# Attention q and k by slices, every second modulation row on VectorE, gates and one value set as channels

## The chip, the cores and the metric

One core of a Trainium2 chip runs the whole program. The metric is device time in microseconds (us), lower is better, and it counts one execution from its start to its end. Five engines work side by side, each through its own list of instructions in a fixed order: TensorE (PE; its weight loads are PEld), VectorE (DVE), ScalarE (ACT), GpSimd (POOL) and SyncE (SP), which issues the large DMAs. An engine whose next instruction has to wait does nothing behind it either.

## The reference

One decoder layer on 256 tokens of width 2048, all in float32. `c` is the conditioning vector.

```python
mod = (silu(c) @ ada_w + ada_b)                      # 2048 x 12288
sh1, sc1, g1, sh2, sc2, g2 = split(mod, 6)
h = rmsnorm(x, norm1_g) * (1 + sc1) + sh1
proj = h @ w_in                                      # 2048 x 5392
aq, ak, av, bq, bk, bv, bz, bb, ba, cq, ck, cv = split(proj)
o_a = dilated_attention(aq, ak, av)                  # 8 heads, three patterns
o_b = gated_deltanet(bq, bk, bv, bz, bb, ba)         # 4 key heads, 8 value heads
o_c = windowed_attention(cq, ck, cv, sinks)          # 8 heads, 2 key/value heads
x = x + g1 * (concat(o_a, o_b, o_c) @ w_out)         # 2048 x 2048
h = rmsnorm(x, norm2_g) * (1 + sc2) + sh2
x = x + g2 * moe(h)                                  # 32 experts, each token uses 2
return rmsnorm(x, final_norm_g)
```

`ada_w` is 100 MB; its first two sixths (sh1, sc1) are needed before anything else, the other four (g1, sh2, sc2, g2, called rows 0 to 3 below) only from the output projection on. The experts' weights are some 400 MB and all are read.

## The kernel before

**Stages.** (1) The slices: the normed input is made and projected in six slices of its 2048 channels (`SLICES`), which need the matching columns of sh1 and sc1 only. In `first`, tiles of `ada_w` (`ada_items`) alternate with tiles of `w_in` (`win_items`, L205). This stage makes only the columns of B (the gated DeltaNet): q, k, v by `chans`, and the 16 gate columns by `gate_columns` when a slice's first tile is at hand. Each slice's part sums are added to an SBUF tile on VectorE (`evac`, L271); the first slice is copied on ScalarE. (2) The rest of `w_in`, 256 columns at a time over all 2048 channels (`win_pair`, two loads of 1 MB each): A's q, k, v (`a_cols`), C's q, k, v (`c_cols`), B's z (`z_cols`). `KINDS` says which columns come out as channels (weights stationary, 256 tokens moving: `w<-stg,hx 128x256`) and which as tokens (`w<-hx,stg`; C's values are 128 wide, so they are matmuls of 128x128). Beside them run the DeltaNet (`delta`, a long chain of small matmuls through PSUM banks of tag "d") and the attention (`attention(0)` for A, `attention(1)` for C). (3) The output projection W_out by `wout_part`, in two halves of its input channels: qs (0, 3) for A's and C's heads and then qs (1, 2) for the DeltaNet's heads. (4) The router, and the experts to the end.

**A weight** is loaded in float32 and made into a high and a low part of float32r by `split` (ScalarE casts, L289; the rest by a subtraction on VectorE or POOL, L290), and each product is three matmuls (`mm3`). In the trace one matmul of a float32 operand is two records.

**The rows.** The four rows g1, sh2, sc2, g2 are 64 tiles of 1 MB (`ada_rows(i, kt)`: row i, channel block kt of 128). `row_tile` (L421 on) does one with four matmuls of 32x512, `prow<-ring,csil`, accumulated over kt in the one bank of tag "r"; after kt = 15 VectorE adds the bank to the SBUF tile `mrow` (L433), and row 2 also makes `n2row` (L435). The loads go through an own stream `st2` with two slots, "rc0" and "rc1" of 1 MB (`side`), which the slices use first and then hand over. `rows_q` lists the tiles row after row; 24 of them are merged with the A columns, 12 with C's, 20 with z's, and the last 8 stand two by two behind the four parts of W_out's first half. `mrow` has to be whole when it is turned for the router (`a<-ident,mrow`), just ahead of W_out's second half.

**What sets the order.** The program is written as a list, and a scheduler with a timeline of its own fixes each engine's order when the kernel is built. Slots and banks are given out in program order: a tile that asks for a bank of a tag waits for the tile that had the bank before it by program order, however far that one's work is put back. `delta()` is called ahead of the merged columns and rows, so that all its "d" banks come ahead of whatever asks for "d" there. `BANKS` gives three banks to "d", three to "w", one each to "a" and "r".

Of the kernel before, what the change touches and what calls it, by code (L numbers as in the profile page):

```python
# [8 lines left out]
F32 = mybir.dt.float32  # L9
# [27 lines left out]

SLICES = [(0, 2), (256, 2), (512, 4), (1024, 4), (1536, 2), (1792, 2)]

PAIRS = [c for a, e in ((O_AQ, O_BQ), (O_CQ, N_IN), (O_BZ, O_BB)) for c in range(a, e, 256)]  # L40

EARLY = ([("ada", s, k0, nk, q) for k0, nk in SLICES for s in range(2) for q in range(nk)]
         + [("b", k0, nk, c) for k0, nk in SLICES for c in range(O_BQ, O_BZ, 2048 // nk)]
         + [("pair", c, h) for c in PAIRS for h in range(2)]
         + [("out", n, q) for n in range(4) for q in range(4)])

# [2 lines left out]
def hybrid_moe(ctx: ExitStack, tc: tile.TileContext, x, c, norm1_g, norm2_g, early, ada_w, ada_b, w_bb,  # L49
# [14 lines left out]
    def mm(o, lhsT, rhs, start=True, stop=True):  # L64
        return T.matmul(o, lhsT, rhs, start=start, stop=stop, skip_group_check=True)  # L65
# [37 lines left out]
    def bank(tag, bufs=None, name=None):  # L103
        return psum.tile([P, 512], F32, name=name or tag, tag=tag, bufs=bufs or BANKS[tag])
# [98 lines left out]

    def win_items(j):
        k0, nk = SLICES[j]  # L205
        return [(early_load("b", k0, nk, c), lambda t, a=(k0, nk, c): win_tile(*a)(t)) for c in range(O_BQ, O_BZ, 2048 // nk)]

    def on(s, items):
        return [(s, load, fn) for load, fn in items]
# [16 lines left out]
    for nk, r in ((4, 4), (2, 8)):  # L226
# [6 lines left out]
        for k0, n in SLICES:  # L233
            if n == nk:
# [8 lines left out]


    CH = [("aq0", 0, 2), ("aq1", 2, 2), ("ak0", 4, 2), ("ak1", 6, 2), ("bq", 8, 4), ("bk", 12, 4),
          ("bv0", 16, 4), ("bv1", 20, 4), ("cq0", 24, 2), ("cq1", 26, 2), ("ck", 28, 1)]
    chan = {}
    K_BZ, K_BB, K_CV = 0, 1024, 1040

    KINDS = [(O_AQ, O_AV, "chan", 0), (O_AV, O_BQ, "av", 0), (O_BQ, O_BZ, "chan", 8), (O_BZ, O_BB, "tok", K_BZ),  # L250
             (O_CQ, O_CV, "chan", 24), (O_CV, N_IN, "tok", K_CV)]

    def ep_tile(tag, n, dt=F32):
        return ep.tile([P, n, NB, P], dt, name=tag, tag=tag)
# [102 lines left out]
    def win_tile(k0, nk, c0):  # L357

        def chans(w, cc, m):

            h = hs[k0]
            p = bank("w")
            for u in range(2):
                for kt in range(nk):
                    mm3(p[:, 256 * u:256 * u + 256], [x[:, kt, cc + P * u:cc + P * (u + 1)] for x in w],
                        [x[:, kt] for x in h], kt == 0, kt == nk - 1)
            t, i = chan[m]
            evac(t[:, i:i + 2].rearrange("p m b t -> p (m b t)"), p, k0)

        def gate_columns():  # L370
            h = hs[k0]
            for b in range(NB):
                p = bank("w")
                for kt in range(nk):
                    mm3(p[:, 0:16], [x[:, kt, P * b:P * (b + 1)] for x in h], [x[:, k0 // P + kt] for x in wbb],
                        kt == 0, kt == nk - 1)
                evac(tok[:, b, K_BB:K_BB + 16], p[:, 0:16], k0)

        def f(t):
            t = t.rearrange("p (k n) -> p k n", k=nk)  # L380
            n = 1024 // nk
            for a in range(0, 2048 // nk, n):
                w = split(t[:, :, a:a + n], nk, 0)
                for z in range(0, n, 256):
                    chans(w, z, 8 + (c0 - O_BQ + a + z) // P)
            if c0 == O_BQ:
                gate_columns()
        return f
# [32 lines left out]


    rowp = {}

    def row_tile(i, kt):
        def f(t):
            if kt == 0:
                rowp[i] = bank("r", name="prow2")
            for g in range(4):
                mm(rowp[i][32 * g:32 * g + 32, :], csil[:, kt, 3 - i:35 - i], t[:, 512 * g:512 * (g + 1)],  # L430
                   start=(kt == 0), stop=(kt == 15))
            if kt == 15:
# [15 lines left out]
            mm(p, identr[q, 32 * g + i:32 * g + i + 1].to_broadcast([32, P]), h[q], start=(j == 0), stop=(j == 1))  # L448


    rows_q = [(ada_rows(i, kt), row_tile(i, kt)) for i in range(4) for kt in range(KT)]

    st2 = Stream()

# [12 lines left out]

    rows_q = on(st2, rows_q)
    a_cols, c_cols, z_cols = ([x for c0 in range(a, e, 256) for x in on(st, win_pair(c0))]
                              for a, e in ((O_AQ, O_BQ), (O_CQ, N_IN), (O_BZ, O_BB)))  # L470
    w_items = [(early_load("out", n, q), None) for qs in ((0, 3), (1, 2)) for n in range(4) for q in qs]
    for s, load, _ in a_cols + c_cols + z_cols + on(st, w_items) + rows_q:
        s.add(load)
# [101 lines left out]
    st.retire(*spare)  # L575
    for s in side:
        st.retire(s, to=st2)
    st.grow((wk, "rx"))
    use(first[-8:])


# [80 lines left out]
    def attention(grp):  # L662
        if grp:
            swap_keys()
            clo = ep_tile("av", 4, F32R)
        for j in range(2):
            ms = (2 * j, 2 * j + 1)
            sd = [attn_scores(grp, m) for m in ms]
            pair = (ep_tile(f"cq{j}", 2, F32R), clo[:, 2 * j:2 * j + 2]) if grp else \
                (ep_tile(f"aq{j}", 2, F32R), ep_tile(f"ak{j}", 2, F32R))  # L670
            for i, m in enumerate(ms):
                mix[m if grp == 0 else 12 + m] = tuple(t[:, i] for t in pair)
                attn_values(grp, m, *sd[i])


    def delta():
# [726 lines left out]
```

## Time and profile before

| | us |
|---|---|
| median of 3 runs | 1641.44 (1640.99 to 1648.26) |
| the profiled execution | 1645.27 |
| its span | 1643.4 |
| delta's last matmuls start | 442.1 |
| last z column ends, W_out starts | 532.4 |
| `mrow` gets its last row | 600.1 |
| `mrow` turned for the router | 604.0 |
| first matmul of an expert | 683.4 |

The page lists busy time by engine, then the span in 40 slices (41 us each). In PE's timeline a row is a start, a duration and a count of records of one form; since matmuls overlap, what a group costs is read from start to the next row's start.

### The profile page before, as it was taken

Reading aid. Unit: us, or ns where it says so; the run is one execution under the profiler, and the core shown is the slowest. Engines: PE = TensorE matmul, PEld = TensorE weight load, DVE = VectorE, ACT = ScalarE, POOL = GpSimd, SP = SyncE. Lnnn points to the kernel's source line nnn. Section 1 sums busy time; section 2 is a strip of 40 time slices with the busy share of each in tenths; the row PEclk is TensorE's granted clock in tenths of the full one; section 3 lists DMA queues with packets and bytes.
Section 4 is the critical chain, followed back from the end, with each engine's and each line's share of the span. In section 5 each row is a group of like instructions: output and inputs, shape, how many; then the busy total and the mean of one; then the engine's idle time right before and its main releaser. Section 6 shows DMA issues by size and latency. Waiting matters only on the chain. (4 is left out here: it accounts for less than half of the span.)

```text
span 1643.4 us, 23829 instructions
## 1 busy us (share of the span) xinstructions
PE 1545.9 (94%) x10064; PEld 945.0 (58%) x10064; DVE 672.1 (41%) x1138; ACT 398.6 (24%) x683; POOL 182.8 (11%) x104
## 2 busy tenths in 40 slices
PE   5899899999999999799999999999999999999895
PEld 3678767898877667544544545445445445445433
DVE  3534854334433544423432533344244234235324
ACT  3323563344345334210110110111011101101102
POOL 1111222352222432000000000000000000000000
PEclk8999999999999999799999999999999999999998
DMA  9986457634589894699999999999999999999995
GB/s 392 408 329 237 162 206 293 246 155 161 225 309 315 308 369 178 232 397 421 420 419 421 421 420 421 421 420 420 421 420 421 420 421 421 421 421 421 420 420 218
DMA packets 82437, 573.76 MB, mean 349 GB/s; under 512 B 9740, under 2 KB 10100, under 8 KB 13336
## 3 DMA queue, kind: packets, MB, share of 16 engines
q1 hardware_dynamic: 82080, 572.02, 86.6%
q8 instruction: 81, 1.33, 0.3%
q10 hardware_dynamic: 248, 0.19, 0.0%
q14 instruction: 28, 0.23, 0.0%
HBM read 570.07 MB, written 2.10 MB: 348 GB/s over the span
## 5 line engine op out<-in xcount | busy, mean ns | idle before, releaser
L65 PE MATMUL u<-ring,xg 128*64 128x512 f32 x2048 | 485.9, 604 | 7.8 <-DMA ring<-in_expert_gu_dram 7.8
L65 PEld LDWEIGHTS u<-ring,xg 128*64 128x64 f32 x2048 | 134.3, 137 | 236.1 <-issue 190.5
L65 PE MATMUL d<-ring,hidT 128*64 128x256 f32 x2048 | 238.1, 382 | 10.5 <-DMA ring<-in_expert_dn_dram 8.9
L65 PE MATMUL w<-hx,stg 128*128 128x256 f32 x1392 | 197.1, 293 | 9.8 <-ACT stg L289 3.1
L65 PEld LDWEIGHTS w<-hx,stg 128*128 128x128 f32 x1392 | 176.6, 194 | 41.8 <-issue 24.3
L65 PEld LDWEIGHTS d<-ring,hidT 128*64 128x64 f32 x2048 | 144.0, 137 | 90.9 <-issue 10.3
L290 POOL TENSOR_TENSOR stg<-ring,stg 128x1024 fp32r<-128x1024 f32 x53 | 128.3, 2421 | 410.5 <-ACT stg L289 367.3
L289 ACT CAST stg<-ring 128x1024 fp32r<-128x1024 f32 x116 | 121.2, 1047 | 187.7 <-PE w L65 152.4
L1190 DVE TENSOR_TENSOR xt<-xt,s 128x512 f32<-128x512 f32 x120 | 82.6, 688 | 165.2 <-PE s L65 164.4
L290 DVE TENSOR_TENSOR stg<-ring,stg 128x1024 fp32r<-128x1024 f32 x63 | 82.2, 1306 | 104.5 <-ACT stg L289 103.7
L1174 DVE SCALAR_TENSOR_TENSOR z<-d,gs,g2b 64x512 f32<-64x512 f32 x120 | 90.0, 750 | 76.1 <-PE d L65 74.2
L65 PE MATMUL prow<-ring,csil 128*32 128x512 f32 (+1 forms) x896 | 113.3, 566 | 0.3 <-DVE csil L180 0.3
L1272 POOL TENSOR_TENSOR xf<-xt,fgb 128x1024 f32<-128x1024 f32 x1 | 2.4, 2377 | 954.9 <-SPq L1289 954.9
L1107 DVE TENSOR_TENSOR xg<-g,sh2c 128x512 f32<-128x512 f32 x64 | 43.6, 691 | 136.8 <-PE u L65 75.7
L65 PEld LDWEIGHTS w<-stg,hx 128*128 128x128 f32 x672 | 83.6, 189 | 22.3 <-issue 18.0
L65 PE MATMUL w<-stg,hx 128*128 128x256 f32 (+1 forms) x672 | 96.1, 288 | 0.0
L1146 ACT ACTIVATE hid<-u 64x512 f32<-64x512 f32 x32 | 18.9, 590 | 286.7 <-PE u L65 276.5
L65 PEld LDWEIGHTS s<-yah,wt 128*128 128x128 f32 x120 | 22.6, 188 | 97.6 <-issue 58.8
L1177 ACT CAST yah<-z 64x512 fp32r<-64x512 f32 x60 | 37.0, 617 | 166.8 <-DVE z L1174 166.8
L1147 DVE TENSOR_TENSOR hid<-hid,u 64x512 f32<-64x512 f32 x32 | 22.1, 690 | 134.0 <-ACT hid L1146 133.8
L65 PE MATMUL g<-oh,h2hi 128*128 128x256 f32 x256 | 70.2, 307 | 5.5 <-DVE xg L1107 4.8
L1121 ACT CAST wt<-t 128x512 fp32r<-128x512 f32 x16 | 9.4, 587 | 233.7 <-PE s L65 222.6
(387 smaller groups left out, 1704.6 us busy)
## 6 DMA issues: line engine op xcount, KB each, us to landing
ring<-in_expert_gu_dram SPq DMA_DIRECT2D x256, 1024.0 KB, 19.8
ring<-in_expert_dn_dram SPq DMA_DIRECT2D x128, 1024.0 KB, 19.8
ring<-in_early_dram SPq DMA_DIRECT2D x90, 1024.0 KB, 8.2
ring<-in_ada_w_dram SPq DMA_DIRECT2D x64, 1024.0 KB, 5.7
xt<-in_x_dram SPq DMA_DIRECT2D x8, 512.0 KB, 6.3
out_dram<-xt SPq DMA_DIRECT2D x8, 256.0 KB, 4.4
fgb<-in_final_norm_g_dram SPq DMA_DIRECT2D x1, 1024.0 KB, 19.8
rw<-in_router_w_dram SPq DMA_DIRECT2D x1, 320.0 KB, 5.2
```

The lines of the kernel that those rows point to most:

```text
L65: return T.matmul(o, lhsT, rhs, start=start, stop=stop, skip_group_check=True)
L289: S.copy(hi, src)
L290: (G if nsplit[0] % GS[part] == GS[part] - 1 else V).tensor_tensor(lo, src, hi, op=ALU.subtract)
L1107: V.tensor_tensor(self.xg[:, 2 * q:2 * q + 2, 0:w], p[:, 0:2 * w].rearrange("p (k s) -> p k s", k=2), sh2c.rearrange("p n k -> p (n k)")[: ...
L1121: S.copy(self.wt.rearrange("p h b t -> p (h b t)"), p)
L1146: S.activation(hid[64:128], p[0:64], AF.Silu)
L1147: V.tensor_tensor(hid[0:64], hid[64:128], p[64:128], op=ALU.mult)
L1174: V.scalar_tensor_tensor(o.rearrange("p (n j) -> p n j", n=m), pd[q, 0:256 * m].rearrange("p (n j) -> p n j", n=m), gs[q, h, u:u + 1], g2h ...
L1177: S.copy(ys[h][q, c], o)
L1190: V.tensor_tensor(x1[n][:, b], x1[n][:, b], p, op=ALU.add)
L1272: G.tensor_tensor(xf, x1[0], fgb[:, None, 0:512].to_broadcast([P, NB, 512]), op=ALU.mult)
```

## The change

- `SLICED`: A's q and k (1024 columns) move from the column stage into the slices: 8 of 1 MB more among the 16 tiles of `w_in` there. They are summed slice by slice through `evac` like B's.
- `gate_columns` makes the gates as channels: 48 matmuls of 16x256 in place of 96 of 128x16, and two transposes in `delta`, which now ask for a "d" bank.
- C's values are channels too (`KINDS`): 48 matmuls of 128x256 in place of 96 of 128x128, and two transposes and a copy in `swap_keys`.
- Rows 0 and 2 are summed on VectorE (`on_dve`): each tile is two operations on 128x1024, a product with the tile's column of `csil` added to an SBUF tile `racc`, which has one buffer. After kt = 15 four matmuls with `onec` sum over the partitions into a bank of tag "d". Rows 1 and 3 stay on PE.
- `rows_q` goes by pairs: rows 0 and 1 alternate, then rows 2 and 3. Attention is a generator in pieces, and the columns, the attention's pieces and the first 56 row tiles are merged evenly. The third extra slot "rx" of the column stream is gone.

```diff
-PAIRS = [c for a, e in ((O_AQ, O_BQ), (O_CQ, N_IN), (O_BZ, O_BB)) for c in range(a, e, 256)]
+PAIRS = [c for a, e in ((O_AV, O_BQ), (O_CQ, N_IN), (O_BZ, O_BB)) for c in range(a, e, 256)]
+SLICED = [(O_BQ, O_BZ), (O_AQ, O_AV)]
...
-    KINDS = [(O_AQ, O_AV, "chan", 0), (O_AV, O_BQ, "av", 0), (O_BQ, O_BZ, "chan", 8), (O_BZ, O_BB, "tok", K_BZ),
-             (O_CQ, O_CV, "chan", 24), (O_CV, N_IN, "tok", K_CV)]
+    KINDS = [(O_AV, O_BQ, "av", 0), (O_BZ, O_BB, "tok", K_BZ), (O_CQ, N_IN, "chan", 24)]
...
         def gate_columns():
             h = hs[k0]
-            for b in range(NB):
-                p = bank("w")
-                for kt in range(nk):
-                    mm3(p[:, 0:16], [x[:, kt, P * b:P * (b + 1)] for x in h], [x[:, k0 // P + kt] for x in wbb],
-                        kt == 0, kt == nk - 1)
-                evac(tok[:, b, K_BB:K_BB + 16], p[:, 0:16], k0)
+            p = bank("w")
+            for kt in range(nk):
+                mm3(p[0:16, 0:256], [x[:, k0 // P + kt] for x in wbb], [x[:, kt] for x in h], kt == 0, kt == nk - 1)
+            evac(bbT, p[0:16, 0:256], k0)
...
+        def on_dve(t):
+            if kt == 0:
+                rowp[i] = wk.tile([P, D], F32, name="racc", tag="racc")
+            acc = rowp[i]
+            for h in range(2):
+                c = slice(1024 * h, 1024 * (h + 1))
+                if kt == 0:
+                    V.tensor_scalar(acc[:, c], t[:, c], csil[:, kt, 3:4], None, op0=ALU.mult)
+                else:
+                    V.scalar_tensor_tensor(acc[:, c], t[:, c], csil[:, kt, 3:4], acc[:, c], op0=ALU.mult, op1=ALU.add)
+            if kt == 15:
+                rowp[i] = bank("d", name="prow2")
+                for g in range(4):
+                    mm(rowp[i][32 * g:32 * g + 32, :], onec[:, 3 - i:35 - i], acc[:, 512 * g:512 * (g + 1)])
+
+        def f(t):
+            (on_pe if i % 2 else on_dve)(t)
             if kt == 15:
                 V.tensor_tensor(mrow, mrow, rowp.pop(i), op=ALU.add)
...
-    rows_q = [(ada_rows(i, kt), row_tile(i, kt)) for i in range(4) for kt in range(KT)]
+    rows_q = [(ada_rows(i, kt), row_tile(i, kt)) for i0 in (0, 2) for kt in range(KT) for i in (i0, i0 + 1)]
...
-    st.grow((wk, "rx"))
...
+        p = bank("a")
+        for b in range(NB):
+            T.transpose(p[:, P * b:P * (b + 1)], head(29)[:, b], ident)
+        S.copy(tok[:, :, K_CV:K_CV + 128], p[:, 0:256].rearrange("p (b n) -> p b n", b=NB))
...
-    use(merge(a_cols, rows_q[0:24]))
-    attention(0)
-    use(merge(c_cols, rows_q[24:36]))
-    attention(1)
-    use(merge(z_cols, rows_q[36:56]))
+    parts = [attention(grp) for grp in range(2)]
+    steps = a_cols + merge(c_cols, parts[:1] * 8) + merge(z_cols, parts[1:] * 8)
+    for step in merge(steps, rows_q[0:56]):
+        if isinstance(step, tuple):
+            use([step])
+        else:
+            next(step)
```

**PE at the end of delta.** `d<-t,qk` is delta's work; the tiles `prow` with `csil` are row tiles, a number for each row's bank (before: 4112 is row 2, 4889 row 3; after: 3279 is row 1, 4285 row 3), and `prow` with `racc` is the finish of a row that VectorE summed (4229 is row 0, 5418 row 2). Before, from delta's last values on:

```order
L65 MATMUL d<-t_2736,Um 128x128 x4
L65 MATMUL w<-stg,hx 128x128 x21
L65 MATMUL prow_4112<-ring,csil 32x512 x5
L65 MATMUL d<-t_2745,qk 128x128 x4
L65 MATMUL prow_4112<-ring,csil 32x512 x3
L65 MATMUL w<-hx,stg 128x256 x12
L65 MATMUL w<-stg,hx 128x128 x24
L65 MATMUL w<-hx,stg 128x256 x12
L65 MATMUL w<-stg,hx 128x128 x24
L65 MATMUL prow_4112<-ring,csil 32x512 x4
L65 MATMUL a<-ck,ident 64x256 x2
L65 MATMUL w<-stg,hx 128x256 x11
```

After, from delta's last values to the start of the second half of A's heads in W_out:

```order
L67 MATMUL d<-t_3195,Um 128x128 x4
L67 MATMUL w<-stg,cq_4869 128x512 x4
L67 MATMUL w<-stg,av 128x512 x2
L67 MATMUL d<-t_3204,qk 128x128 x4
L67 MATMUL prow_4229<-racc,onec 32x512 x4
L67 MATMUL prow_4285<-ring,csil 32x512 x4
L67 MATMUL w<-t_5066,identr 128x512
L67 MATMUL w<-t_5067,identr 128x512
L67 MATMUL w<-stg,aq_3697 128x512 x2
```

The finish of row 0 stands right behind delta's last matmuls, and the first tile of row 3 behind that; the last tile of row 1 stands 167 rows of this list further up. Between them there is no row tile. In the kernel before row tiles stand all along.

**PE at the end of W_out's first half.** Names with bq, bk, bv are the second half's (one of its four parts stands ahead). Before, the last two row tiles; `a<-ident,mrow` comes 12 rows of the list further on:

```order
L65 MATMUL w<-stg,bq 128x512
L65 MATMUL prow_4889<-ring,csil 32x512 x4
L65 MATMUL w<-stg,bq 128x512
L65 MATMUL w<-stg,bk 128x512
L65 MATMUL w<-stg,bq 128x512 x2
L65 MATMUL w<-stg,bk 128x512
L65 MATMUL w<-stg,bq 128x512
L65 MATMUL prow_4889<-ring,csil 32x512 x4
L65 MATMUL w<-stg,bq 128x512 x2
```

After, up to the turn of `mrow`:

```order
L67 MATMUL w<-stg,bv_5009 128x512
L67 MATMUL w<-stg,bv_5008 128x512 x2
L67 MATMUL w<-stg,bv_5009 128x512
L67 MATMUL prow_4285<-ring,csil 32x512 x28
L67 MATMUL prow_5418<-racc,onec 32x512 x4
L67 MATMUL prow_4285<-ring,csil 32x512 x8
L67 MATMUL a<-ident,mrow 128x4 x4
L67 MATMUL w<-g1hl,identr 128x512 x4
L67 MATMUL a<-rsum,ones 128x40
```

Nine tiles of row 3 (28 matmuls, then 8) and the finish of row 2 now stand in one block between the two halves. Seven tiles stand further up, the first where the piece above shows it, the six others in W_out's first half.

**SP, the queue of the loads, at the start of W_out.** `in_ada_w` are the row tiles' loads, `in_early` those of columns and W_out, `in_x` the input once more. Before:

```order
L188 DMA ring<-in_ada_w_dram 128x2048 [waits DMAHW4_49,PE_49]
L188 DMA ring<-in_ada_w_dram 128x2048 [waits DMAHW5_49,DMAHW0_49,PE_49]
L185 DMA ring<-in_early_dram 128x2048 [waits DVE_49,Pool_49]
L944 DMA xt_5118<-in_x_dram 128x2x512 [waits PE_49]
L944 DMA xt_5119<-in_x_dram 128x2x512 [waits DMAHW3_49,PE_49]
L188 DMA ring<-in_ada_w_dram 128x2048 [waits DMAHW7_49,PE_49]
L944 DMA xt_5120<-in_x_dram 128x2x512 [waits PE_49]
L188 DMA ring<-in_ada_w_dram 128x2048 [waits DMAHW6_49,DMAHW0_49,PE_49]
```

After:

```order
L980 DMA xt_5001<-in_x_dram 128x2x512 [waits PE_49]
L187 DMA ring<-in_early_dram 128x2048 [waits DMAHW4_49,DVE_49,Pool_49]
L187 DMA ring<-in_early_dram 128x2048 [waits DMAHW5_49,DVE_49,Pool_49]
L187 DMA ring<-in_early_dram 128x2048 [waits DMAHW6_49,DVE_49,Pool_49]
L190 DMA ring<-in_ada_w_dram 128x2048 [waits DVE_49]
L190 DMA ring<-in_ada_w_dram 128x2048 [waits DMAHW7_49,PE_49]
L190 DMA ring<-in_ada_w_dram 128x2048 [waits DMAHW6_49,DMAHW0_49,DVE_49]
L190 DMA ring<-in_ada_w_dram 128x2048 [waits DMAHW7_49,DMAHW1_49,PE_49]
L190 DMA ring<-in_ada_w_dram 128x2048 [waits DMAHW2_49,DMAHW0_49,DVE_49]
L187 DMA ring<-in_early_dram 128x2048 [waits DMAHW3_49,DVE_49,Pool_49]
L190 DMA ring<-in_ada_w_dram 128x2048 [waits DMAHW4_49,DMAHW1_49,PE_49]
L190 DMA ring<-in_ada_w_dram 128x2048 [waits DMAHW5_49,DMAHW2_49,DVE_49]
```

Before, each row load waits for PE alone. After, the first of the 30 last row loads stands behind the loads of x, and the loads wait for DVE and PE in turn: each of the two slots is loaded again when its own row's engine is done with it.

## Rows read from the trace of the kernel before

**Rows 1.** The page: share of the span by engine; GB/s of DMA in 40 slices.

```profile
span 1643.4 us, 23829 instructions
...
PE 1545.9 (94%) x10064; PEld 945.0 (58%) x10064; DVE 672.1 (41%) x1138; ACT 398.6 (24%) x683; POOL 182.8 (11%) x104
...
GB/s 392 408 329 237 162 206 293 246 155 161 225 309 315 308 369 178 232 397 421 420 419 421 421 420 421 421 420 420 421 420 421 420 421 421 421 421 421 420 420 218
```

**Rows 2.** Stretches of 50 us: busy us and count by engine, granted clock, DMA share.

```profile
core 0: us, PE busy (x) PEld busy (x) DVE busy (x) ACT busy (x) POOL busy (x), PEclk, DMA share, GB/s
...
200.00:250.00 50.00, 45.68 (x305) 32.67 (x306) 30.61 (x49) 30.40 (x50) 14.39 (x8) 0.97 0.61 211
...
550.00:600.00 50.00, 50.00 (x243) 30.36 (x242) 18.64 (x23) 16.40 (x18) 14.39 (x6) 1.00 0.86 315
600.00:650.00 50.00, 50.00 (x233) 37.68 (x234) 22.78 (x32) 23.82 (x35) 17.41 (x8) 1.00 0.65 252
```

**Rows 3.** PE in order of time, around delta's last matmuls: start us, us.

```profile
442.13 1.16 PE L65 MATMUL d<-t,qk 128*128 128x128 f32 x8
...
449.83 2.79 PE L65 MATMUL w<-stg,hx 128*128 128x128 f32 x24
452.55 1.07 PE L65 MATMUL prow<-ring,csil 128*32 128x512 f32 x8
453.55 0.65 PE L65 MATMUL a<-ck,ident 128*64 128x256 f32 x4
...
464.07 3.30 PE L65 MATMUL w<-stg,hx 128*128 128x256 f32 x26
467.31 0.92 PE L65 MATMUL a<-ck,cq 64*128 64x128 f32 x4
```

**Rows 4.** PE in order of time: gate columns; W_out matmuls; mrow turned.

```profile
185.50 1.40 PE L65 MATMUL w<-wbb,hx 128*128 128x16 f32 x12
187.64 7.91 PE L65 MATMUL w<-hx,stg 128*128 128x256 f32 x52 [0.73 <-DVE bk L271]
...
532.43 0.40 PE L65 MATMUL w<-stg,aq 128*128 128x512 f32 x1
...
591.08 0.40 PE L65 MATMUL w<-stg,av 128*128 128x512 f32 x1
591.32 0.40 PE L65 MATMUL w<-stg,cq 128*128 128x512 f32 x1
...
603.96 0.95 PE L65 MATMUL a<-ident,mrow 128*128 128x4 f32 x8
```

**Rows 5.** All uses of mrow, 190 to 700 us: ns min/median/max, first and last start.

```profile
L433 DVE TENSOR_TENSOR mrow<-mrow,prow x4: 675/684/689, 292.0 to 600.1; 128x512 f32<-128x512 f32 x4
```

**Rows 6.** Issues of the row loads, by window: KB, median us to landing.

```profile
ring<-in_ada_w_dram SPq DMA_DIRECT2D x1, 1024.0 KB, 4.7
...
ring<-in_ada_w_dram SPq DMA_DIRECT2D x8, 1024.0 KB, 5.0
...
ring<-in_ada_w_dram SPq DMA_DIRECT2D x16, 1024.0 KB, 5.6
...
ring<-in_ada_w_dram SPq DMA_DIRECT2D x10, 1024.0 KB, 6.5
```

**Rows 7.** Groups on VectorE, 190 to 700 us: busy us, mean ns of one.

```profile
L290 DVE TENSOR_TENSOR stg<-ring,stg 128x1024 fp32r<-128x1024 f32 x42 | 54.7, 1302 | 100.3 <-ACT stg L289 99.6 <-PE prow L65 0.6
...
L1060 DVE SCALAR_TENSOR_TENSOR h2lo<-xa,r,h2hi 128x512 fp32r<-128x512 f32 x8 | 5.7, 747 | 1.0 <-ACT h2hi L1009 1.0
```

**Rows 8.** VectorE and POOL in order of time, 194 us on.

```profile
194.58 2.29 DVE L696 SCALAR_TENSOR_TENSOR ct<-bk,cw,ct 128x255 f32<-128x255 f32 x1 [0.20 <-ACT ct L691]
...
201.06 0.47 DVE L696 SCALAR_TENSOR_TENSOR ct<-bk,cw,ct 128x254 f32<-128x254 f32 x1
...
194.22 2.38 POOL L290 TENSOR_TENSOR stg<-ring,stg 128x1024 fp32r<-128x1024 f32 x1 [5.04 <-ACT stg L289]
```

**Rows 9.** A stretch at the router's end: columns as in Rows 2.

```profile
677.00:683.00 6.00, 5.67 (x26) 5.67 (x27) 2.29 (x5) 0.59 (x1) 0.00 (x0) 0.50 0.25 107
```

More of the change, by code (lines that the diff above doesn't have):

```diff
@@ L38 @@
 SLICES = [(0, 2), (256, 2), (512, 4), (1024, 4), (1536, 2), (1792, 2)]
-PAIRS = [c for a, e in ((O_AQ, O_BQ), (O_CQ, N_IN), (O_BZ, O_BB)) for c in range(a, e, 256)]
+PAIRS = [c for a, e in ((O_AV, O_BQ), (O_CQ, N_IN), (O_BZ, O_BB)) for c in range(a, e, 256)]
+SLICED = [(O_BQ, O_BZ), (O_AQ, O_AV)]
 EARLY = ([("ada", s, k0, nk, q) for k0, nk in SLICES for s in range(2) for q in range(nk)]
-         + [("b", k0, nk, c) for k0, nk in SLICES for c in range(O_BQ, O_BZ, 2048 // nk)]
+         + [("b", k0, nk, c) for k0, nk in SLICES for a, e in SLICED for c in range(a, e, 2048 // nk)]
          + [("pair", c, h) for c in PAIRS for h in range(2)]
@@ L205, in win_items @@
         k0, nk = SLICES[j]
-        return [(early_load("b", k0, nk, c), lambda t, a=(k0, nk, c): win_tile(*a)(t)) for c in range(O_BQ, O_BZ, 2048 // nk)]
+        return [(early_load("b", k0, nk, c), lambda t, a=(k0, nk, c): win_tile(*a)(t)) for s, e in SLICED for c in range(s, e, 2048 // nk)]
     def on(s, items):
@@ L245, in hybrid_moe @@
     CH = [("aq0", 0, 2), ("aq1", 2, 2), ("ak0", 4, 2), ("ak1", 6, 2), ("bq", 8, 4), ("bk", 12, 4),
-          ("bv0", 16, 4), ("bv1", 20, 4), ("cq0", 24, 2), ("cq1", 26, 2), ("ck", 28, 1)]
+          ("bv0", 16, 4), ("bv1", 20, 4), ("cq0", 24, 2), ("cq1", 26, 2), ("ck", 28, 1), ("cv", 29, 1)]
     chan = {}
     K_BZ, K_BB, K_CV = 0, 1024, 1040
-    KINDS = [(O_AQ, O_AV, "chan", 0), (O_AV, O_BQ, "av", 0), (O_BQ, O_BZ, "chan", 8), (O_BZ, O_BB, "tok", K_BZ),
-             (O_CQ, O_CV, "chan", 24), (O_CV, N_IN, "tok", K_CV)]
+    KINDS = [(O_AV, O_BQ, "av", 0), (O_BZ, O_BB, "tok", K_BZ), (O_CQ, N_IN, "chan", 24)]
     def ep_tile(tag, n, dt=F32):
@@ L259, in hybrid_moe @@
             chan[m0 + i] = (t, i)
+    bbT = ep.tile([P, 256], F32, name="bbT")[0:16]
     av = ep.tile([P, NB, 512], F32, name="av", tag="av")
@@ L384, in f @@
                 for z in range(0, n, 256):
-                    chans(w, z, 8 + (c0 - O_BQ + a + z) // P)
+                    chans(w, z, (c0 + a + z) // P - (O_BQ // P - 8 if c0 >= O_BQ else 0))
             if c0 == O_BQ:
@@ L423, in hybrid_moe, with on_pe @@
     rowp = {}
+    onec = ep.tile([P, 36], F32, name="onec")
+    V.memset(onec, 0.0)
+    V.memset(onec[:, 3:4], 1.0)
     def row_tile(i, kt):
-        def f(t):
+        def on_pe(t):
             if kt == 0:
@@ L469, in hybrid_moe @@
     a_cols, c_cols, z_cols = ([x for c0 in range(a, e, 256) for x in on(st, win_pair(c0))]
-                              for a, e in ((O_AQ, O_BQ), (O_CQ, N_IN), (O_BZ, O_BB)))
+                              for a, e in ((O_AV, O_BQ), (O_CQ, N_IN), (O_BZ, O_BB)))
     w_items = [(early_load("out", n, q), None) for qs in ((0, 3), (1, 2)) for n in range(4) for q in qs]
@@ L667, in attention @@
             ms = (2 * j, 2 * j + 1)
-            sd = [attn_scores(grp, m) for m in ms]
+            sd = []
+            for m in ms:
+                sd.append(attn_scores(grp, m))
+                yield
             pair = (ep_tile(f"cq{j}", 2, F32R), clo[:, 2 * j:2 * j + 2]) if grp else \
@@ L673, in attention @@
                 attn_values(grp, m, *sd[i])
+                yield
     def delta():
@@ L701, in delta @@
         conv(1)
+        pt = bank("d")
+        for b in range(NB):
+            T.transpose(pt[:, 16 * b:16 * (b + 1)], bbT[:, P * b:P * (b + 1)], ident[0:16, 0:16])
+        V.tensor_copy(tok[:, :, K_BB:K_BB + 16], pt[:, 0:32].rearrange("p (b n) -> p b n", b=NB))
         bb = tok[:, :, K_BB:K_BB + 8]
@@ L946, in hybrid_moe @@
     g1hl = halves(scratch(dt=F32R), scratch(dt=F32R), mrow)
-    st.retire((wk, "rx"))
     for n in range(4):
```

## The prediction

> **What bounds the kernel now.** I read the page first. PE is busy for 94% of the span, and from about 700 us on the DMA line stands at 420 GB/s to the end [rows 1]: from there the experts' weights set the pace, whatever PE does. A change ahead of the experts can therefore only move their start, and moves the end by as much. Ahead of them I read stretches of 50 us. PE is full at 550 to 650 (50.00 of 50), while the DMA share is 0.86 and 0.65 [rows 2]; PE is what binds there, and work taken off it would count in full. Around 200 to 250 PE is short by 4.3 us while VectorE is busy for 30.6 of 50 [rows 2]. Last I looked for the point that everything has to pass: `mrow` gets its fourth row at 600.1 [rows 5] and is turned for the router at 603.96, when PE comes to it [rows 4]. So the rows are just in time now: PE is the later of the two by 3 us. What is to be forecast is the time of this turn in the new order.
>
> **Part 1, the work on PE.** One row tile costs PE 1.00 us (452.55 to 453.55, [rows 3]). 32 tiles leave, and two finishes of four float32 matmuls come, which I bound at a tile each: -30. Gates: 96 small matmuls at 0.117 (12 in 1.40) [rows 4] are 11.2; 48 of 256 columns at 0.125 (26 in 3.24) [rows 3] are 6.0: -5. C's values: 96 at 0.113 (24 in 2.72) are 10.9, 48 at 0.125 are 6.0, transposes 0.3: -4.6 [rows 3]. A's q and k are the same matmuls at another place: 0. That is -40 on PE, and with nothing else the kernel would run 1601.
>
> **Part 2, where delta ends.** The rows pile up, and the order shows where. Row 0 is summed in `racc`, but its finish asks for a "d" bank, and all of delta's "d" banks come ahead of it by program order; so the finish stands right behind delta's last matmuls. Until it ran, row 1 can't be added to `mrow`, bank "r" isn't free for row 3, and `racc`, with one buffer, isn't free for row 2. In the kernel before, delta ended at 442 [rows 3], long before W_out. In the new order it ends later: all the column work stands ahead of that point, and of W_out 48 matmuls, 0.24 us each (591.08 to 591.32) [rows 4]. When does PE get there? W_out started at 532.4 [rows 4]; ahead of it were 52 row tiles, and ahead of the new point stand 16, all of row 1. So 532 + 48 x 0.24 (11.5) - 36 x 1.00 - 10 (gates and values) + 1 (attention pieces that stood behind) = 499. VectorE gets 16 tiles and some 20 sums in a stretch where PE already waits at times, so I add 3: **502**. Bounds: 492 if the waits of 200 to 250 (4.3 us) and as much again go away; 515 if VectorE holds PE up by 16.
>
> **Part 3, the rows behind it.** From there 15 tiles each of rows 2 and 3 are still to be loaded, over two slots. By the queue's waits one slot always carries row 2 and is loaded again when VectorE is done, the other row 3, when PE is done; the loads stand in turn in one queue, so the slower pair sets both. A cycle is one landing and one VectorE pass, one after the other, since a slot can't be filled while it is read. Landing: medians between 4.7 and 6.5 us; I take 5.5, between the 5.0 and 5.6 of windows with an equal traffic [rows 6]. VectorE: two operations on 128x1024. The trace has none of this kind; the nearest by size and by number of inputs is 1.30 us, and the same kind on 128x512 takes 0.75, which is 1.5 for twice as much [rows 7]. I take 1.3, as sizes agree there: 2.6 a tile, bounds 2.4 and 3.0. So a cycle is **8.1 us**, bounds 7.1 and 9.5. PE has its own say on the first six: tiles 1 to 6 of row 3 stand between W_out's matmuls, the sixth 53 us of packed PE work behind the start, 8.8 a tile. Sum: 502 + 2 (finish on PE, 0.68 for the add [rows 5]) + 2.6 (first tile on VectorE) = 507; the sixth tile is done at 556 by PE's order and at 507 + 6 x 8.1 = 556 by the loads. Nine cycles more, for which PE has no other work ahead: 73, so 629. Then the finish of row 2 (2 us), behind which the last tiles of row 3 stand; the load of the very last waits for the one before it, and five other loads of 1 MB stand ahead of it in the queue: one landing of 5.5 and some of theirs, 10, bounds 5 and 16. One tile and the add: 2. `mrow` is whole at **643** and turned at once, against 604 now: +39.
>
> **Part 4, behind the turn.** One part of W_out's second half is done ahead of it, so what follows is shorter by 4 us (54 against 58 with each matmul at its price above). On the other side PE does one tile of 1 us in 8 through the block of nine tiles. After an idle stretch it was granted 0.50, the level of 1.2 GHz, for the six busy microseconds 677 to 683 [rows 9]; at half speed 6 us are 3 of work lost: +3. W_out's second half then runs as before, and the experts start 39 - 4 + 3 = 38 us later. The working goes by the span of 1643.4 of the profiled execution (1645.3); as a difference it goes on the median of 1641.4: **1679**. By the bounds: 492 + 5 + 53 + 9 x 7.1 + 2 + 5 + 2 = 623 turned, +19 - 4 = +15, 1656; and 515 + 5 + 6 x 9.5 + 9 x 9.5 + 2 + 16 + 2 = 683, +79 - 4 + 6 = +81, 1722. The 40 us that PE is spared are in this sum: they are why the block begins at 502 and not at 540; PE then waits them away, and more.
>
> **Two rules beside it.** A VectorE operation on 128x255 took 2.29 us beside a POOL operation of 2.38 us that began 0.36 before; its neighbour on 128x254 took 0.47 [rows 8]. The Trainium skill (SBUF - State Buffer, "SBUF: two separate sides") says that such a pair excludes each other on a shared port for the whole instruction, which speaks against rows on VectorE while POOL makes low parts; the trace agrees. By that rule each meeting would cost up to 1.9 us, and the cycle with one meeting would be 10. On landings the same page ("The DMA setup-cost knee") has about 2 us and 436 GB/s, an estimate of 4.4 us for 1 MB and a cycle of 7.0; the trace has 4.7 to 6.5, and it decides.
>
> **The rivals.** *VectorE late in the first part.* 16 tiles are 42 us of VectorE beside its conv and low parts between 190 and 330; 200 to 250 has it 61% busy and PE waiting [rows 2]. If that and meetings with POOL [rows 8] hold PE up by 18 more, the block begins at 520: **1697**. For it: the operations that stretch to 2.3. Against: where VectorE has less than half of its time taken, as from 550 on, PE is full [rows 2]. *The loads stream.* If landings of the two slots overlap with VectorE's passes down to what DMA can carry, a pair of 2.1 MB at 421 GB/s [rows 1] is 5.0 us: 502 + 54 + 45 + 9 = 610 turned, **1646**, no change. Against: the waits in the queue name the engine that read the same slot. It decides below a cycle of about 5.5. *The rows are spread, as the change says.* If the finish of row 0 doesn't wait for delta's end, because the bank is had sooner than the names in the order tell me, rows 2 and 3 run among the columns and all 40 us of PE count, less some 10 for VectorE: **1611**, faster. Place: the end of row 0 on VectorE. It would have to run by about 455 in place of 502 for the turn to come no later than now. Against it: PE goes through a fixed list, and the finish stands behind delta in it.
>
> **How the numbers follow.** Forecast 0.74 (1656 to 1722 by its bounds, most of it below 1708), VectorE late 0.12, loads stream 0.08, rows spread 0.06. A measurement of this kernel can tell about 0.5%, 8 us, from no change. Faster by more: the last case, 0.06. Within: the streaming case and the forecast's lowest end, 0.10. Slower: 0.84. The range of 8 in 10 leaves out the fast case, half of the no-change case and the top end: 1646 to 1708.
>
> **What would show it.** In the new trace: delta's last `d<-t,qk` at about 500 and `prow<-racc,onec` right behind; row loads in pairs about 8 us apart from then to 630; nine tiles of row 3 on an otherwise idle PE between W_out's halves; the add to `mrow` at about 643; an expert's first matmul at about 721. Wrong would be: the finish of row 0 well before 480 (part 2), pairs under 7 us apart (part 3), PE busy with W_out in that block, or a shift of the experts' start that the end doesn't follow.

## The result and the profile after

| | before | after |
|---|---|---|
| median of 4 runs, us (lowest to highest) | 1641.3 (1641.0 to 1648.3) | 1690.2 (1686.4 to 1694.3) |
| ratio to before (95% interval) | | 1.028 (1.025 to 1.032) |
| span of the profiled execution | 1643.4 | 1685.7 |
| delta's last matmuls start | 442.1 | 495.2 |
| `mrow` turned for the router | 604.0 | 648.0 |
| an expert's first matmul | 683.4 | 726.2 |

The kernel is 2.8% slower. The page of the changed kernel (its span; busy time by engine; GB/s in 40 slices):

```profile
span 1685.7 us, 23233 instructions
...
PE 1519.6 (90%) x9732; PEld 931.2 (55%) x9732; DVE 766.8 (45%) x1223; ACT 397.2 (24%) x678; POOL 181.1 (11%) x101
...
GB/s 394 360 352 254 232 296 241 299 237 76 76 178 308 327 284 175 176 287 421 420 421 420 420 421 421 420 420 421 421 420 421 420 421 421 421 420 421 421 421 231
```

PE is busy 26 us less than in [rows 1] and the span is 42 us longer. On both pages the last 22 slices are the tail at some 420 GB/s (the very last one is full only in part), and the end moved by 42.3 where the first matmul of an expert moved by 42.8. So the loss lies wholly ahead of the experts. The stretches of 50 us (columns as in [rows 2]):

```profile
200.00:250.00 50.00, 43.84 (x327) 36.49 (x326) 47.59 (x78) 28.98 (x38) 14.14 (x5) 0.93 0.73 270
250.00:300.00 50.00, 47.07 (x319) 38.02 (x319) 42.69 (x75) 32.40 (x62) 16.00 (x9) 0.93 0.66 241
...
550.00:600.00 50.00, 26.14 (x110) 14.09 (x109) 23.23 (x19) 6.29 (x6) 7.86 (x3) 0.71 0.82 310
600.00:650.00 50.00, 15.03 (x61) 3.81 (x58) 13.47 (x14) 1.24 (x2) 0.00 (x0) 0.50 0.79 301
```

Where [rows 2] had PE full at 550 to 650, it now has 26.1 and 15.0 of 50, at a mean granted clock of 0.71 and then 0.50, which is the level of 1.2 GHz throughout. Neither VectorE (23 and 13) nor DMA (0.82 and 0.79) is full there either: that is the mark of a chain in which each waits for the other. PE's timeline shows its beginning (start us, us, what, and in brackets idle time before):

```profile
495.17 1.05 PE L67 MATMUL d<-t,qk 128*128 128x128 f32 x8
496.15 1.06 PE L67 MATMUL prow<-racc,onec 128*32 128x512 f32 x8
502.20 1.94 PE L67 MATMUL prow<-ring,csil 128*32 128x512 f32 x8 [4.99 <-DVE mrow L454]
```

These are delta's last matmuls, the finish of row 0 right behind them, and the first tile of row 3, which waited 5 us for `mrow` to take rows 0 and 1. VectorE's row 2 in the same execution:

```profile
499.48 1.41 DVE L443 TENSOR_SCALAR racc<-ring,csil 128x1024 f32<-128x1024 f32 x2
...
507.03 2.47 DVE L445 SCALAR_TENSOR_TENSOR racc<-ring,csil,racc 128x1024 f32<-128x1024 f32 x2
...
521.57 4.61 DVE L445 SCALAR_TENSOR_TENSOR racc<-ring,csil,racc 128x1024 f32<-128x1024 f32 x2 [0.99 <-DMA ring<-in_ada_w_dram]
...
531.08 4.25 DVE L445 SCALAR_TENSOR_TENSOR racc<-ring,csil,racc 128x1024 f32<-128x1024 f32 x2 [1.37 <-DMA ring<-in_ada_w_dram]
...
555.67 2.48 DVE L445 SCALAR_TENSOR_TENSOR racc<-ring,csil,racc 128x1024 f32<-128x1024 f32 x2
...
610.85 2.48 DVE L445 SCALAR_TENSOR_TENSOR racc<-ring,csil,racc 128x1024 f32<-128x1024 f32 x2 [4.86 <-DMA ring<-in_ada_w_dram]
618.14 2.48 DVE L445 SCALAR_TENSOR_TENSOR racc<-ring,csil,racc 128x1024 f32<-128x1024 f32 x2 [4.82 <-DMA ring<-in_ada_w_dram]
625.43 2.48 DVE L445 SCALAR_TENSOR_TENSOR racc<-ring,csil,racc 128x1024 f32<-128x1024 f32 x2 [4.81 <-DMA ring<-in_ada_w_dram]
```

After the first tile, 15 more follow one after another from 507 to 628; ahead of each of the last VectorE is idle for 4.8 us until its load has landed. PE's end of the block, and the queue of the loads at the same time:

```profile
614.33 1.94 PE L67 MATMUL prow<-ring,csil 128*32 128x512 f32 x8 [4.92 <-DMA ring<-in_ada_w_dram]
621.22 1.94 PE L67 MATMUL prow<-ring,csil 128*32 128x512 f32 x8 [4.96 <-DMA ring<-in_ada_w_dram]
626.87 2.17 PE L67 MATMUL prow<-racc,onec 128*32 128x512 f32 x6 [3.71 <-DVE racc L445]
...
645.25 1.93 PE L67 MATMUL prow<-ring,csil 128*32 128x512 f32 x8 [13.65 <-DMA ring<-in_ada_w_dram]
647.99 1.87 PE L67 MATMUL a<-ident,mrow 128*128 128x4 f32 x8 [0.81 <-DVE mrow L454]
```

```profile
627.94 1.97 SPq L187 DMA_DIRECT2D ring<-in_early_dram  x4
629.97 0.46 SPq L193 DMA_DIRECT2D ring<-in_expert_gu_dram  x1
631.64 0.33 SPq L190 DMA_DIRECT2D ring<-in_ada_w_dram  x1
```

PE does one tile of row 3 in 7 us, each after 4.9 us of waiting; then the last load of all, issued at 631.6 behind five others of 1 MB, lands 13.6 us later, and `mrow` is turned at 648.0, where [rows 4] has 604.0.

### The profile page after: what moved, and what is told of

Read it like the earlier page. It is cut to its first block, busy times and chain, and to the rows that moved or that the text cites. A ratio compares the mean times of both kernels' runs of the same rounds, so it can differ in the third digit from the quotient of the medians.

```text
span 1685.7 us, 23233 instructions
## 1 busy us (share of the span) xinstructions
PE 1519.6 (90%) x9732; PEld 931.2 (55%) x9732; DVE 766.8 (45%) x1223; ACT 397.2 (24%) x678; POOL 181.1 (11%) x101
## 3 DMA queue, kind: packets, MB, share of 16 engines
q8 instruction: 78, 1.28, 0.3%
## 5 line engine op out<-in xcount | busy, mean ns | idle before, releaser
L67 PE MATMUL prow<-ring,csil 128*32 128x512 f32 (+1 forms) x640 | 88.1, 597 | 56.6 <-DMA ring<-in_ada_w_dram 51.4
L445 DVE SCALAR_TENSOR_TENSOR racc<-ring,csil,racc 128x1024 f32<-128x1024 f32 x60 | 83.4, 1429 | 48.2 <-DMA ring<-in_ada_w_dram 48.2
L292 DVE TENSOR_TENSOR stg<-ring,stg 128x1024 fp32r<-128x1024 f32 x66 | 85.8, 1300 | 38.7 <-ACT stg L291 38.6
L67 PE MATMUL w<-stg,hx 128*128 128x256 f32 x576 | 88.1, 299 | 0.1
L67 PEld LDWEIGHTS w<-stg,hx 128*128 128x128 f32 x576 | 75.3, 196 | 10.5 <-issue 6.1
```

What stands on the lines that cost most here:

```text
L292: (G if nsplit[0] % GS[part] == GS[part] - 1 else V).tensor_tensor(lo, src, hi, op=ALU.subtract)
L445: V.scalar_tensor_tensor(acc[:, c], t[:, c], csil[:, kt, 3:4], acc[:, c], op0=ALU.mult, op1=ALU.add)
```

## The experiments

All ratios are to the kernel before, run on the same chip beside each, with a 95% interval.

**One word: the finish in another bank.** Attention takes tag a a piece at a time, delta keeps tag d to its end.

```diff
-                rowp[i] = bank("d", name="prow2")
+                rowp[i] = bank("a", name="prow2")
```

> The changed kernel with one word different: the finish of rows 0 and 2 takes its PSUM bank from tag a, which attention uses a piece at a time, in place of tag d, which delta holds to its end. Pile-up theory: the finish of row 0 runs at about 330 to 350 us in place of 496, rows 2 and 3 run among the columns, mrow is turned for the router before 575 instead of 648, and all of the 40 us that PE was spared come out: 1600 to 1612 us, against 1690 for the change and 1641 before. Rival (VectorE is the cost: the row sums hold up its other work, PE waits for that): VectorE has the same work here as in the change, so the time stays at 1670 to 1690.

Measured: 1614.2 us, ratio 0.982 (0.978 to 0.986). Run a second time: 1615.4, 0.981 (0.979 to 0.983), as expected below. The turn of `mrow` and the adds to it in the first of the two (ns, then first and last start):

```profile
L67 PE MATMUL a<-ident,mrow x8: 168/253/253, 559.4 to 560.1; 128*128 128x4 f32 x8
L454 DVE TENSOR_TENSOR mrow<-mrow,prow x4: 683/686/689, 381.7 to 554.9; 128x512 f32<-128x512 f32 x4
```

The first row is added at 382 in place of 499 and the turn is at 559 in place of 648. VectorE has the same operations as in the change, and delta's last matmuls come later here than there (504.0 against 495.2), so it is not a shorter delta that helped. So the pile-up is shown as the cause of the loss: some 76 us hung on which bank the finish asks for (1690 against 1614). Of the numbers expected, the turn came ahead of 575 as said, the finish of row 0 was 30 to 50 us later than said, and the time 2 us above the range: some 30 us came out by the ratio and not all of the 40.

> The run with the other bank once more, on the same chip as the one without slices and as the spreading alone, so that the three can be compared: about 0.982 of the kernel before, 1608 to 1616.

**All rows on PE.** The other parts of the change stay.

```diff
-            (on_pe if i % 2 else on_dve)(t)
+            on_pe(t)
...
-    rows_q = [(ada_rows(i, kt), row_tile(i, kt)) for i0 in (0, 2) for kt in range(KT) for i in (i0, i0 + 1)]
+    rows_q = [(ada_rows(i, kt), row_tile(i, kt)) for i in range(4) for kt in range(KT)]
```

> The changed kernel with all four rows on PE, one row after the other as before; all other parts of the change stay. Pile-up theory: no row asks for a bank of tag d, nothing piles up, and what is left is the 10 us of gates and values: about 1632 us (1625 to 1640). Rival (the loss is from q and k in the slices or from the even spreading of attention): it stays above 1660. Rival (VectorE is the cost): also about 1632, so this run does not part that one from the pile-up; the run with the other bank does.

Measured: 1635.9 us, 0.994 (0.992 to 0.996), as expected; the rival that puts the loss on the slices or the spreading wanted more than 1660. With the run above it also prices the rows on VectorE where they don't pile up: 0.981 against 0.994, 21 us of the 30 that PE is spared. The rest comes back as waits of PE. The stretches 200 to 300, first of the run with all rows on PE and then of the second one with bank a:

```profile
200.00:250.00 50.00, 48.61 (x388) 38.62 (x389) 38.21 (x75) 33.91 (x46) 10.83 (x5) 1.00 0.74 263
250.00:300.00 50.00, 49.38 (x357) 38.95 (x354) 31.64 (x59) 29.59 (x61) 16.88 (x10) 1.00 0.55 206
```

```profile
200.00:250.00 50.00, 43.81 (x327) 36.46 (x327) 47.76 (x78) 28.98 (x38) 13.88 (x5) 0.93 0.74 271
250.00:300.00 50.00, 44.57 (x304) 35.23 (x305) 41.54 (x74) 30.76 (x57) 14.16 (x8) 0.97 0.65 232
```

PE is short by 2.0 us of 100 there with VectorE busy for 70, and by 11.6 with VectorE busy for 89.

**The rows alone, in the kernel before.** The third extra slot "rx" of the column stream goes with them, as in the change.

```diff
+        def on_dve(t):
...
+                rowp[i] = bank("d", name="prow2")
...
+            (on_pe if i % 2 else on_dve)(t)
...
+    rows_q = [(ada_rows(i, kt), row_tile(i, kt)) for i0 in (0, 2) for kt in range(KT) for i in (i0, i0 + 1)]
...
-    st.grow((wk, "rx"))
...
```

> The kernel before with the row part of the change alone: rows 0 and 2 on VectorE, by pairs, finish in tag d; no other part. The rows pile up behind delta here too, but delta ends at about 425 us in this order, 70 us ahead of where it ends in the change. Pile-up theory: 15 cycles of 7.3 to 8 us and the tail end at about 560, PE comes to the turn of mrow at about 576 (604 less 28), so the pile-up is hidden nearly whole and the time is 1612 to 1632, faster than before. Rival (VectorE is the cost): the same VectorE work makes this one slower than before too, 1655 to 1685.

Measured: 1671.7 us, 1.016 (1.012 to 1.021): slower, as the rival said, so the expectation failed. Two of its numbers were wrong. VectorE's row 2 in this run:

```profile
466.15 4.61 DVE L445 SCALAR_TENSOR_TENSOR racc<-ring,csil,racc 128x1024 f32<-128x1024 f32 x2
...
475.78 4.14 DVE L445 SCALAR_TENSOR_TENSOR racc<-ring,csil,racc 128x1024 f32<-128x1024 f32 x2 [3.55 <-DMA ring<-in_ada_w_dram]
...
505.83 2.48 DVE L445 SCALAR_TENSOR_TENSOR racc<-ring,csil,racc 128x1024 f32<-128x1024 f32 x2
...
529.58 2.48 DVE L445 SCALAR_TENSOR_TENSOR racc<-ring,csil,racc 128x1024 f32<-128x1024 f32 x2
...
540.41 2.83 DVE L445 SCALAR_TENSOR_TENSOR racc<-ring,csil,racc 128x1024 f32<-128x1024 f32 x2
...
607.84 2.48 DVE L445 SCALAR_TENSOR_TENSOR racc<-ring,csil,racc 128x1024 f32<-128x1024 f32 x2 [4.79 <-DMA ring<-in_ada_w_dram]
615.21 2.48 DVE L445 SCALAR_TENSOR_TENSOR racc<-ring,csil,racc 128x1024 f32<-128x1024 f32 x2 [4.89 <-DMA ring<-in_ada_w_dram]
622.55 2.48 DVE L445 SCALAR_TENSOR_TENSOR racc<-ring,csil,racc 128x1024 f32<-128x1024 f32 x2 [4.86 <-DMA ring<-in_ada_w_dram]
```

The block began at 453, where PE came to delta's end, and not at 425; and its tiles came 9 to 24 us apart as long as column and W_out loads stood between the row loads in the same queue. Only the last three are 7.3 apart, as at the end of the block in the change. The wait named most often for the queue ahead of such a load, after those for the row operations, is the making of low parts on VectorE (41 us in 11 waits between 450 and 630): each in-order load of another stream holds the row loads behind it. How much of the time is the rival's, and how much the pile-up's, the next run shows, one word apart.

```diff
-                rowp[i] = bank("d", name="prow2")
+                rowp[i] = bank("a", name="prow2")
```

> The kernel before with the row part alone, and the finish in tag a in place of tag d: one word apart from the run that took 1667 to 1672. The rows came too late there, at 628 in place of the 560 expected: the block began at 453 and its first ten cycles took 9 to 14 us. Pile-up theory: without the wait for delta the rows spread, PE is 30 us shorter, and VectorE costs some 8 us of waits as in the run with the other bank: 1611 to 1622. Rival (what made that run slow is VectorE, where two row operations took 4.6 us in place of 2.5 beside POOL): VectorE has the same work, so it stays above 1655.

Measured: 1636.1 us, 0.995 (0.993 to 0.997), between the two. The turn and the adds here:

```profile
L65 PE MATMUL a<-ident,mrow x8: 168/252/253, 590.2 to 590.9; 128*128 128x4 f32 x8
L454 DVE TENSOR_TENSOR mrow<-mrow,prow x4: 672/678/687, 409.4 to 587.0; 128x512 f32<-128x512 f32 x4
```

The turn is at 590 with bank a, and was at 629 with bank d: the same word takes 35 us out here too (1.016 against 0.995). But of the 30 us spared on PE only 8 are left. Between 150 and 600 PE's busy time is 22.6 us short of full, against 8.6 in the kernel before: 14 us come back as waits, not the 8 expected. By the trace VectorE ended 14.7 us of PE's waits in that stretch, 6.9 before; the others ended with ScalarE, POOL and loads. So VectorE is a second cost, smaller than the pile-up. How much of the 14 us is due to the missing slot "rx" is open: no run takes that slot away alone. The remaining 8 of the 22 us that were lost are not in these waits.

**A third slot.** The finish stays in bank d; the column stream gives one of its three slots to the rows.

```diff
-    for s in side:
+    for s in side + main[2:]:
         st.retire(s, to=st2)
```

> The changed kernel with one of the three slots of the column stream handed to the row stream, which so has three slots in place of two; the finish still waits for delta's end. Two-slot theory: the block still begins at about 500, but a load no longer waits for the slot that its own row has just left, so the cycle of a pair in the late block falls from 7.3 to what DMA carries, 5.0 to 5.5 (2.1 MB at 421 GB/s), and the last load no longer stands behind five others: mrow is turned at about 605 in place of 648 and the time is 1640 to 1655. Rival (a cycle is bound by VectorE's pass or by the DMA rate as it is): the cycle stays above 7 and the time above 1675.

Measured: 1662.9 us, 1.011 (1.009 to 1.014); the profiled execution has a span of 1654.2. VectorE's row 2 late in the block, the turn, and the stretch in between; behind it the like stretch of the change:

```profile
583.28 2.48 DVE L445 SCALAR_TENSOR_TENSOR racc<-ring,csil,racc 128x1024 f32<-128x1024 f32 x2 [3.39 <-DMA ring<-in_ada_w_dram]
589.09 2.48 DVE L445 SCALAR_TENSOR_TENSOR racc<-ring,csil,racc 128x1024 f32<-128x1024 f32 x2 [3.33 <-DMA ring<-in_ada_w_dram]
595.44 2.48 DVE L445 SCALAR_TENSOR_TENSOR racc<-ring,csil,racc 128x1024 f32<-128x1024 f32 x2 [3.87 <-DMA ring<-in_ada_w_dram]
601.78 2.48 DVE L445 SCALAR_TENSOR_TENSOR racc<-ring,csil,racc 128x1024 f32<-128x1024 f32 x2 [3.86 <-DMA ring<-in_ada_w_dram]
607.12 2.48 DVE L445 SCALAR_TENSOR_TENSOR racc<-ring,csil,racc 128x1024 f32<-128x1024 f32 x2 [2.85 <-DMA ring<-in_ada_w_dram]
```

```profile
L67 PE MATMUL a<-ident,mrow x8: 252/252/273, 613.9 to 614.7; 128*128 128x4 f32 x8
```

```profile
565.00:605.00 40.00, 14.89 (x69) 4.10 (x71) 16.39 (x14) 0.00 (x0) 0.00 (x0) 0.61 0.98 361
```

```profile
575.00:628.00 53.00, 13.81 (x62) 1.61 (x63) 18.78 (x15) 0.00 (x0) 0.34 (x1) 0.53 0.83 312
```

The cycle falls from 7.3 to 6.0, the DMA share rises from 0.83 to 0.98, and the turn comes at 614 in place of 648. So with two slots it was the round trip that set the pace. With three, DMA is all but full, though at 361 GB/s and not at the 421 expected, for which no run shows the reason; that and a time of 1663 in place of 1655 at most are the misses. It isn't a pure test of the slot: the last row load also no longer stands behind five others, which is about 16 of the 34 us (20 us from the end of row 2 to the turn in the change, 4 here).

**The other parts, each alone in the kernel before.** First gates and C's values as channels (`gate_columns`, `KINDS`):

```diff
...
-             (O_CQ, O_CV, "chan", 24), (O_CV, N_IN, "tok", K_CV)]
+             (O_CQ, N_IN, "chan", 24)]
...
```

> The kernel before with gates and C's values as channels, no other part. By the sum PE is 10 us shorter and nothing waits for it longer: 1630 to 1638, about 0.6% faster. Rival: the matmuls with 16 or 128 columns hid weight loads or waits that show now, no change within 3 us.

Measured: 1636.0 us, 0.9935 (0.992 to 0.995), 10.7 us faster, as the sum had it (10). Then A's q and k in the slices:

```diff
...
-         + [("b", k0, nk, c) for k0, nk in SLICES for c in range(O_BQ, O_BZ, 2048 // nk)]
+         + [("b", k0, nk, c) for k0, nk in SLICES for a, e in SLICED for c in range(a, e, 2048 // nk)]
...
```

> The kernel before with A's q and k in the slices, no other part. By the sum the same matmuls at another place, and 20 sums of 0.68 us more on VectorE in a stretch where PE waited for it already: 0 to 5 us slower, 1641 to 1650. Rival (the slices' PE waits grow by what VectorE has more, 14 us): 1655.

Measured: 1651.8 us, 1.0046 (1.003 to 1.007), 8 us slower, 3 more than expected at most. And the even spreading of attention and rows (`parts`, `merge(steps, rows_q[0:56])`):

> The kernel before with attention in pieces and columns, pieces and rows merged evenly, no other part. By the sum no work is added or taken away: 1636 to 1644. From the runs so far (all but rows -0.6%, gates and values -0.65%, slices +0.46%) about -0.4% is left for it, 1634 to 1640. Rival: it costs, 1645 to 1655.

Measured: 1661.0 us, 1.008 (1.005 to 1.011), 13 us slower: the rival, and by its time even above the rival's range. `mrow` is turned at 621.7 there, with PE busy nearly all the way. The parts don't add: gates, slices and spreading alone come to +0.6%, and together, as the run with all rows on PE has them (there without the slot "rx"), to -0.6%. Why the spreading alone costs so much I did not settle.

**Two tries at more.** With bank a, another order of the rows:

```diff
-    rows_q = [(ada_rows(i, kt), row_tile(i, kt)) for i0 in (0, 2) for kt in range(KT) for i in (i0, i0 + 1)]
+    rows_q = [(ada_rows(i, kt), row_tile(i, kt)) for i, kt in [(1, kt) for kt in range(KT)] + [(i, kt) for kt in range(KT) for i in (0, 3)] + [(2, kt) for kt in range(KT)]]
```

> The changed kernel with the finish in tag a and another order of the rows: row 1 on PE first, all 16 tiles, then rows 0 (VectorE) and 3 (PE) by turns, then row 2 on VectorE. It moves VectorE's 42 us of row 0 out of the stretch 200 to 300, where PE waited 9 us in the run with the other bank, to 300 and later, where VectorE was busy for 40%. If those waits are VectorE's row sums, they fall to about 2 us as in the run with all rows on PE, and the time is 1600 to 1612, 5 to 10 less than the run with the other bank. Rival: row 2, alone on VectorE at the end, comes in too late (16 tiles at 4.7 to 5 us or more) and takes it back: 1612 to 1630.

Measured: 1625.2 us, 0.987 (0.985 to 0.989), the rival: slower than the same kernel with the rows in pairs (0.981). The stretches 200 to 250 and 500 to 550:

```profile
200.00:250.00 50.00, 49.17 (x389) 38.97 (x389) 38.70 (x76) 33.60 (x46) 10.28 (x5) 1.00 0.72 260
500.00:550.00 50.00, 36.75 (x158) 26.69 (x158) 49.27 (x41) 16.81 (x22) 16.55 (x6) 0.97 0.78 281
```

The early waits are gone (49.2 of 50, against 43.8 with the rows in pairs). That fits the row operations as their cause but does not show it alone, since PE also has 15 row tiles of its own between 200 and 300 now, 9 with the rows in pairs. The 16 tiles of row 2 now lie late, most of them beside W_out, where VectorE is busy for 49.3 of 50 and PE for 36.8. And with bank a, A's q and k back among the columns:

```diff
...
-SLICED = [(O_BQ, O_BZ), (O_AQ, O_AV)]
...
```

> The changed kernel with the finish in tag a, and A's q and k back in the column stage; gates, values, rows and the spreading of attention stay. The slices alone cost 0.46% (7 us) in the kernel before, and with the rows on VectorE PE waited 9 us between 200 and 300 for sums and row operations. If the parts add, 1602 to 1610, better than 1614 with the slices. Rival: q and k in the slices gave cover to the start of delta in the full change, so that without them delta's chain stands ahead of PE with less other work beside it, and the time is the same or up to 10 us worse, 1614 to 1625.

Measured: 1629.3 us, 0.990 (0.988 to 0.992), 14 us worse than with the slices, and 4 above the rival's range. The slices cost time alone and save time in company; the cover they may give to delta's start is argued, not shown. The version with bank a and nothing else is the best of all, 1.9% faster than the kernel before.

## Why the prediction was right

Forecast 1679, range 1646 to 1708, measured 1690. The mechanism was as forecast, and read off the order: a finish behind delta, 15 tiles of two rows behind that, two slots. That the turn came within 5 us of its forecast is in part luck: start -6, the six cycles beside W_out +8, the nine behind -3 and the tail +6 cancel in part. By its steps:

- **Where delta ends (part 2).** Forecast 502, measured 496.2. The packed sum alone was 499, and its term for PE's work was 3 us short: up to this point PE is busy for 36.6 us less than before up to W_out's start, where the sum had 33.4. The 3 us added for VectorE did not come in the total: PE waited longer between 200 and 300 (9.1 us, before 4.3) but less between 50 and 150 (1.2, before 5.6), so that it was idle for 32.9 us in all, before 32.6. The lower bound of 492 comes to 490 by the terms that it names (499 less twice 4.3); nothing hangs on it. After, then before:

```profile
0.00:496.15 496.15, 463.24 (x3649) 390.49 (x3649) 285.80 (x481) 228.58 (x409) 142.71 (x84) 0.97 0.66 250
```

```profile
0.00:532.43 532.43, 499.79 (x3966) 401.40 (x3966) 236.28 (x439) 223.13 (x407) 135.43 (x84) 0.97 0.70 264
```

- **The cycle (part 3).** Forecast 8.1 throughout. The six beside W_out took 57 us from the first tile's end (500.9) to the seventh's (558.2), 49 forecast; the nine behind took 70, 73 forecast. The sum was 5 us off and the parts more. Alone a cycle is 7.3: 4.8 of waiting for the landing and 2.48 of VectorE, so both 5.5 and 2.6 were high. Beside W_out it is 9.5, and the trace has three things there that the sum had not: the queue stood 12.0 us in five waits ahead of W_out's loads, which hold the row loads behind them; VectorE's pass was stretched to 4.61 and 4.25 where POOL was making a low part; and in three of the six cycles (507.03, 514.18, 555.67) VectorE did not wait for a load but came late from its other work. What each of them is worth alone no run shows.
- **The tail (part 3).** 14 forecast from the end of row 2 to the turn, 20 measured. The load of the last tile took 13.6 us behind the five others, where I had 10, with 16 as the bound: all five had just been issued.
- **Behind the turn (part 4).** 78.2 us from the turn to the experts, 79.4 before: -1.2, forecast -1. The end followed the experts' start within half a microsecond.
- **The sum.** Turn 648.0 (643 forecast), experts 726.2 (721), span +42.3 (+38). The medians differ by 49, the profiled executions by 42: the profiled one was 4 us above the median before and 3 below it after, and those 7 us of the gap to the forecast have no place in the traces.
- **The rivals.** *VectorE late* did not hold PE up by 18, but the runs with bank a show that it costs: 21 of 30 us are left of the rows in the one, 8 of 30 in the other (there without the slot "rx"). *Rows spread, as the change says* was priced at 1611 and came to 1614 when the bank let it; since the parts behind it don't add, part of that nearness is luck. *Loads stream* decides below a cycle of 5.5; three slots reached 6.0.

**The shared port.** Beside the 4.61 us at 521.57 in VectorE's rows above, POOL had this one:

```profile
522.53 2.57 POOL L292 TENSOR_TENSOR stg<-ring,stg 128x1024 fp32r<-128x1024 f32 x1 [3.63 <-ACT stg L291]
```

Two operations that take 2.48 together elsewhere took 4.61, and POOL's took 2.57 within that time. The Trainium skill (SBUF - State Buffer, "SBUF: two separate sides") has such a pair, a VectorE operation with two SBUF inputs and a GpSimd (POOL) operation that reads SBUF, exclude each other for the whole instruction; the trace agrees, with 2.1 us lost here. In the first run with bank a the mean of a row operation is 1.54 against a median of 1.28, and each stretched one overlaps a POOL operation.

## What to carry to other kernels

When a new user of a rotating buffer is put behind a long-lived one in program order, its work waits for the end of that one, however early its inputs are there; look for it in each engine's fixed order before adding up what the engines are spared. Where a stretch shows no engine and no DMA full, count slots: with as many slots as rows in turn, landing and use add up, and one slot more than that lets them overlap. Work that is taken off a full engine comes back in part as waits for the one that gets it, so price it from the stretch where it lands.

## What the runs showed of the hardware that I had not expected

The first tile of a row needs one tensor input and a column, and took 0.74 us on 128x1024; from the second tile on, with two tensor inputs, it took 1.26 to 1.28. I had priced both at 1.3.

```profile
L445 DVE SCALAR_TENSOR_TENSOR racc<-ring,csil,racc x60: 1258/1279/3409, 199.4 to 626.6; 128x1024 f32<-128x1024 f32 x60
...
L443 DVE TENSOR_SCALAR racc<-ring,csil x4: 743/744/2870, 186.6 to 500.1; 128x1024 f32<-128x1024 f32 x4
```
